# Attention scores with the second pass (q hi by K lo) as pairs of 64-row matmuls

## The chip, the cores and the metric

The kernel runs on one core of one Trainium2 chip. The metric is the device time of one execution in microseconds; a kernel's figure is the median of its runs.

## The reference, cut to what matters

Two residual blocks of a first kind run one after the other (1024 tokens, width 1024), then one block of a second kind (gated linear attention and a convolutional feed-forward). The change lies in the attention of the first kind, which is computed twice, once per layer:

```python
def gqa_axial_attention(q, k, v, qn_g, kn_g, tables):
    q = rmsnorm(q.reshape(b, s, H_B, HEAD_DIM), qn_g)      # 8 heads of 64
    k = rmsnorm(k.reshape(b, s, KV_HEADS, HEAD_DIM), kn_g) # 2 key heads of 64
    q = apply_axial_rope(q, tables)
    k = apply_axial_rope(k, tables)
    def attend(qblk):                                       # a block of 128 queries
        sc = jnp.einsum('bqkgd,bskd->bkgqs', qblk, k).astype(jnp.float32) * scale
        p = jax.nn.softmax(sc, axis=-1).astype(v.dtype)
        return jnp.einsum('bkgqs,bskd->bqkgd', p, v)
```

Everything is float32. For each block of 128 queries there are 2 key heads with 4 query heads each, and each of these 8 heads has a score matrix of 128 queries by 1024 keys.

## The kernel before, in words

**Numbers in two halves.** TensorE multiplies in the type fp32r. So that little is lost, the kernel writes a float32 number as a sum of two fp32r numbers, hi and lo (`split`, L71: a cast, on VectorE or ScalarE, and a subtraction on VectorE, L76 by way of L57), and adds up the products of the parts.

**The scores.** `qs` holds, for each head, 64 columns of q hi and 64 of q lo side by side (`split_q`, L411). A transpose of the 128 columns gives `qT`: rows 0 to 63 are q hi, rows 64 to 127 q lo (`prep_turn`, L414). `Kst` holds K hi (index 0) and K lo (index 1), each twice, in rows 0 to 63 and again in rows 64 to 127. So one matmul of 128 rows with K hi gives (q hi + q lo) by K hi, and a second one with K lo adds (q hi + q lo) by K lo. A score matrix `S` is 128 by 1024 floats in PSUM; there are two buffers of it. It takes four matmuls of 128x512: two column halves, each with K hi and then K lo (L476). Then VectorE takes the maximum of each row (`nm`, L481), ScalarE the exponential with a running sum (L66), which goes to SBUF and sets the buffer of `S` free.

**The loop.** Inside a layer the attention runs over g = 0 to 15 (8 query blocks qt by 2 key heads kv; g = 2 qt + kv), and for each g over eight units u0 to u7 (L591 and L598). In unit u TensorE does, in this order:

- `turn` (L493): four 128x128 transposes of exponentials of g into a PSUM tile named `tr`; ScalarE casts the tile to hi, VectorE subtracts for lo (tiles `X`);
- one piece of `scores(g+1)` (L467), as far as the next `yield`;
- at u2 `gate` (L510): two more transposes into a `tr` tile, which VectorE multiplies into `gb` (L517);
- at u1 `prep_turn` of g+2: four transposes into a `tr` tile, copied to `qT` by ScalarE;
- three matmuls of 128x512 of the output projection of the query block before (`project`, L547; tile `o`); when a column half is full, ScalarE squares it and VectorE multiplies it (`tmp`); after the second half `ss`, `ve`, a power on GpSimd (`rs`), and a VectorE operation over 128x1024 (`xt`, L567);
- at u7 of odd g `turn_ya`: four transposes into a `tr` tile;
- four matmuls of 128x256 with V (`attend`, L519; tile `po`), for the unit three earlier; after the last of eight, at u2 and u6, ScalarE copies half of `po` to `ol`, and VectorE adds (`ol`) and multiplies (`gb`).

**Who sets the order.** The order on TensorE is that of the program (L79, `manual_schedule`). On VectorE and ScalarE a scheduler sets it when the program is built, and the engine then runs its queue strictly in that order. There are two `tr` buffers for all the uses above; they are handed out in turn, so that transposes into a `tr` tile must wait until the reader of the tile two before is done. Only in the first query block do some units use the tile `o` in place of `tr` (L498).

Before the loop, `scores(0)` runs between pieces of `gate_b` (L574).

Of the kernel before, what the change touches and what calls it, by code (L numbers as in the profile page):

```python
# [11 lines left out]
AF = mybir.ActivationFunctionType  # L12
ALU = mybir.AluOpType
AX = mybir.AxisListType
# [22 lines left out]
def build(tc, a):  # L37
# [5 lines left out]
    nc = tc.nc  # L43
    seq = [0]

    def T(pool, shape, tag, dt=F32, bufs=None):
        seq[0] += 1
        return pool.tile(shape, dt, tag=tag, name=f"{tag}_{seq[0]}", bufs=bufs)

    def opened(stack, name, side="left"):  # L50
        return stack.enter_context(tc.tile_pool(name=name, bufs=1, side=side, reuse_waits="tile"))

    def opened_psum(stack, name):
        return stack.enter_context(tc.tile_pool(name=name, bufs=1, space=PSUM, reuse_waits="tile"))

    def tt(out, in0, in1, op, eng=None):
        (eng or nc.vector).tensor_tensor(out=out, in0=in0, in1=in1, op=op)  # L57
# [4 lines left out]
    def mm(out, lhsT, rhs, start, stop):  # L62
        nc.tensor.matmul(out, lhsT, rhs, start=start, stop=stop)  # L63

    def act(out, in_, func, **kw):
        nc.scalar.activation(out=out, in_=in_, func=func, **kw)  # L66
# [4 lines left out]
    def split(hi, lo, src, on_act=False):  # L71
        if on_act:
            nc.scalar.copy(hi, src)  # L73
        else:
            nc.vector.tensor_copy(hi, src)
        tt(lo, src, hi, ALU.subtract)  # L76
# [21 lines left out]
    def bcast(p, src, n, tag, bufs=1):  # L98
        t = T(p, [128, n], tag, bufs=bufs)
        load(t, src.broadcast_to([128, n]))  # L100
        return t
# [3 lines left out]
    def quarter(i, dt=F32R):  # L105

        return T(xpool, [128, 4096], f"X{i}", dt)
# [125 lines left out]
    for l in range(2):  # L233
        sP = ExitStack()
        psL = opened_psum(sP, f"psA{l}")
# [16 lines left out]
        if l == 0:  # L252
# [8 lines left out]
            for _ in range(2):  # L261
                for e in range(2):
                    r = identr[64 * e:64 * e + 64]
# [80 lines left out]
        Kst = T(pR, [128, 2, 2, 1024], "K", F32R)  # L344
# [6 lines left out]
        for i, nm, sc in ((1, "k_norm_g", 1.0), (0, "q_norm_g", 0.125)):  # L351
            g = bcast(pT, a[nm][l:l + 1, :], 64, "g64")
# [47 lines left out]
        qTs, qss = {}, {}  # L400

        def use_q(t, ps):
            qr = T(pT, [128, 512], "t1", bufs=2)
            rope(qr, T(pT, [128, 512], "sq", bufs=2), T(pT, [128, 512], "qn", bufs=2), ps, 8, 0, t)
            if t == 0:
                qss[0] = T(pT, [128, 8, 2, 64], "qs", F32R)
                split_q(0, qr)
            else:
                load(tok(q_d, t), qr)

        def split_q(qt, q):  # L411
            split(qss[qt][:, :, 0], qss[qt][:, :, 1], q.rearrange("p (h d) -> p h d", d=64))

        def prep_turn(g):  # L414
            qt, kv = divmod(g, 2)
# [31 lines left out]
        psL = opened_psum(sB, f"psB{l}")  # L447
        pB = opened(sB, f"pB{l}", "right")
        pQ = opened(sB, f"pQ{l}", "right")
        g_post = bcast(cst, a["post_g"][l:l + 1, :], 1024, "gpost")  # L450
        g_pre = bcast(cst, a["pre_g"][1:2, :] if l == 0 else a["norm1"], 1024, "gpre")
        XB = [x[:, j] for x in (quarter(i, F32).rearrange("p (u k) -> p u k", u=4) for i in (2, 3)) for j in range(4)]
        qf, ya = XB[7][:, 0:512], XB[7][:, 512:1024]
        count = [0, 0]
        Ps, gbs, pos, yTs = {}, {}, {}, {}
# [11 lines left out]
        def scores(g):  # L467

            qt, kv = divmod(g, 2)
            sm = T(pQ, [128, 4], "sm", bufs=3)  # L470
            P = {}
            for hh in (0, 2, 1, 3):
                ps = T(psL, [128, 1024], "S", bufs=2)
                for c in range(2):
                    for s in range(2):
                        mm(ps[:, 512 * c:512 * c + 512], qTs[g][:, hh],  # L476
                           Kst[:, s, kv, 512 * c:512 * c + 512], s == 0, s == 1)
                    if c == 0:
                        yield
                nm = T(pQ, [128, 1], "nm", bufs=4)  # L480
                nc.vector.reduce_max(out=nm, in_=ps, axis=AX.X, negate=True)  # L481
                P[hh] = XB[count[1] % 7]
                count[1] += 1
                act(P[hh], ps, AF.Exp, bias=nm, accum_out=sm[:, hh:hh + 1])
                if hh == 3:
                    ri = T(pQ, [128, 4], "ri", bufs=3)
                    nc.vector.reciprocal(ri, sm)
                    rb = T(pQ, [128, 4, 64], "rb")
                    nc.vector.tensor_copy(rb, ri.unsqueeze(2).broadcast_to([128, 4, 64]))
                    Ps[g] = P, rb  # L490
                yield

        def turn(g, u):  # L493

# [79 lines left out]
        for i, _ in enumerate(scores(0)):  # L574
            next(units[i // 4])
# [15 lines left out]
        for g in range(2 * NT):  # L591
            qt, kv = divmod(g, 2)
# [54 lines left out]
    cols = T(pG, [128, 3], "cols")  # L647
# [23 lines left out]
    def gmm(n=512, tag="mm"):  # L671
        return T(psG, [128, 512], tag, bufs=2)[:, 0:n]
# [86 lines left out]
    for h in range(4):  # L759
# [11 lines left out]
        for t in range(NT):  # L771
            if h == 0 and t == 6:
                alpha_low()
            ps = gmm(256, ("mm", "po")[t % 2])
# [15 lines left out]
        for hf in range(2):  # L790
            ps = gmm().rearrange("p (t i) -> p t i", t=4)
# [22 lines left out]
        for hf in range(2):  # L814
            ps = gmm().rearrange("p (t i) -> p t i", t=4)
# [16 lines left out]
        for t in range(NT):  # L832
            ps = gmm(256)
# [124 lines left out]
    for t in range(NT):  # L958
# [8 lines left out]
        for c in range(2):  # L967
            ps = T(psH, [128, 512], "mm", bufs=4)
# [227 lines left out]
    for c in range(2):  # L1196
        ps = [T(psD, [128, 512], f"d{t}") for t in range(NT)]
# [115 lines left out]
```

## Time and profile before

| | us |
|---|---|
| median of 3 runs | 2218.72 (2218.39 to 2222.95) |
| the profiled execution | 2216.28 |
| its span, first to last instruction | 2214.5 |
| TensorE matmuls busy in the span | 2185.2 (99%), 11919 matmuls |
| VectorE busy | 1511.8 (68%) |
| ScalarE busy | 927.5 (42%) |
| granted TensorE clock | 1.0 of full speed in all 40 slices |

The busy shares are means over the whole program. The two attention loops lie at about 279 to 530 us and 820 to 1072 us of the span, and for the change these stretches count: the transposes of `turn` and the score matmuls occur only there (the first score tile, before the loop, at 259 us). A matmul's busy time in the profile runs from its start to a modelled end, and matmuls overlap, so the price of one in a stream is the distance from its start to the next one's start.

### The profile page before, as it was taken

What the parts mean: (1) busy time and instruction counts of PE and PEld (TensorE: products, weight loads), DVE (VectorE), ACT (ScalarE), POOL (GpSimd) and SP (SyncE); (2) the same over time, 40 slices, a digit from 0 to 9 for tenths busy, and PEclk for the clock granted to TensorE, in tenths of its full rate; (3) what the DMA queues carried; (4) which work ended last, traced back from release to release, by engine and by line L of the source; (5) the groups of instructions that cost most, each with busy time, mean ns of one, the idle gap of its engine ahead of it and who ended that gap; (6) DMA issues with size and microseconds to landing.
All of it is one profiled execution on the core that took longest, in us unless ns stands there. A gap on an engine that the chain in (4) does not pass through costs nothing.

```text
span 2214.5 us, 30128 instructions
## 1 busy us (share of the span) xinstructions
PE 2185.2 (99%) x11919; PEld 1871.3 (85%) x11919; DVE 1511.8 (68%) x2307; ACT 927.5 (42%) x1631; POOL 157.1 (7%) x210
## 2 busy tenths in 40 slices
PE   8999999999999999999999999999999999999998
PEld 7888888888788878888889999988888888888887
DVE  7545688888844568888865555647998888763434
ACT  4203266666210326666643223223544444442323
POOL 1004200000100510000001001100000000000000
PEclk9999999999999999999999999999999999999999
DMA  5131411112423150111331111343222222264443
GB/s 196 62 120 39 148 39 63 44 53 90 144 68 105 39 162 25 58 48 49 113 108 49 53 57 63 107 161 107 77 86 86 86 81 81 77 225 147 147 148 122
DMA packets 74541, 206.52 MB, mean 93 GB/s; under 512 B 8736, under 2 KB 21408, under 8 KB 74400
## 3 DMA queue, kind: packets, MB, share of 16 engines
q1 hardware_dynamic: 73392, 200.93, 26.7%
q10 hardware_dynamic: 1008, 3.67, 0.6%
q8 instruction: 93, 1.52, 0.3%
q14 instruction: 48, 0.39, 0.1%
HBM read 160.01 MB, written 44.56 MB: 92 GB/s over the span
## 4 chain that ended last, share of the span: by engine, by line
PE 57%; DVE 5%; POOL 2%; issue 1%; ACT 1%; DMA 1%; POOLq 0%; SPq 0%; ACTq 0%; DVEq 0%
PE mm L63 13%; PE d L63 11%; PE a L1016 10%; PE b L1016 8%; PE po L63 5%; PE o L63 3%; PE S L63 3%; PE tr L504 2%; POOL rs L57 1%; DVE X L57 1%; POOL sq L57 1%; PE tr L154 1%; DVE w L57 0%; PE big L63 0%; PE tr L63 0%
## 5 line engine op out<-in xcount | busy, mean ns | idle before, releaser
L63 PE MATMUL mm<-w,X 128*128 128x512 f32 (+1 forms) x3072 | 550.6, 337 | 3.9 <-DVE w L57 1.8
L63 PEld LDWEIGHTS mm<-w,X 128*128 128x128 f32 x3072 | 475.5, 189 | 64.9 <-DVE w L57 2.6
L57 POOL TENSOR_TENSOR rs<-ve,nhalf 128x1 f32<-128x1 f32 (+2 forms) x136 | 109.6, 806 | 2025.1 <-DVE ve L93 2018.1
L63 PE MATMUL d<-w,X 128*128 128x512 f32 x1056 | 239.9, 389 | 0.1
L63 PEld LDWEIGHTS d<-w,X 128*128 128x128 f32 x1056 | 198.1, 188 | 41.7 <-DVE X L57 0.5
L57 DVE TENSOR_TENSOR X<-tr,X 128x512 fp32r<-128x512 f32 x296 | 201.5, 683 | 38.3 <-ACT X L73 35.3
L73 ACT CAST X<-tr 128x512 fp32r<-128x512 f32 x296 | 171.2, 585 | 114.2 <-PE tr L504 77.9
L57 DVE TENSOR_TENSOR w<-raw,w 128x1024 fp32r<-128x1024 f32 (+1 forms) x155 | 183.0, 1182 | 27.5 <-ACT w L73 26.5
L63 PE MATMUL S<-K,qT 128*128 128x512 f32 x512 | 179.0, 430 | 2.8 <-DVE t L60 1.6
L481 DVE TENSOR_REDUCE nm<-S 128x1 f32<-128x1024 f32 x128 | 155.7, 1217 | 25.5 <-PE S L63 25.1
L63 PEld LDWEIGHTS po<-X,V 128*128 128x128 f32 x1024 | 151.6, 189 | 22.8 <-DVE ol L57 6.8
L63 PE MATMUL po<-X,V 128*128 128x256 f32 x1024 | 167.6, 287 | 1.9 <-DVE ol L57 1.8
L66 ACT ACTIVATE X<-S,nm 128x1024 f32<-128x1024 f32 x128 | 143.0, 1117 | 62.0 <-DVE nm L481 61.8
L63 PE MATMUL mm<-X,w 128*128 128x512 f32 x672 | 155.5, 390 | 0.0
L1016 PE MATMUL a<-X,w 128*128 128x512 f32 x624 | 150.6, 393 | 0.8 <-DVE s L57 0.8
L504 PE MATMUL tr<-ident,X 128*128 128x128 f32 x960 | 144.7, 273 | 4.7 <-ACT qT L420 2.1
L63 PEld LDWEIGHTS mm<-X,w 128*128 128x128 f32 x672 | 125.3, 188 | 25.5
L57 DVE TENSOR_TENSOR X<-yr,X 128x1024 fp32r<-128x1024 f32 x44 | 53.6, 1221 | 135.1 <-ACT X L73 135.1
L1016 PEld LDWEIGHTS a<-X,w 128*128 128x128 f32 x624 | 117.1, 188 | 27.8 <-DVE s L57 1.3
L504 PEld LDWEIGHTS tr<-ident,X 128*128 128x128 f32 x960 | 110.6, 139 | 12.4 <-DVE X L57 3.9
L73 ACT CAST X<-yr 128x1024 fp32r<-128x1024 f32 x44 | 45.9, 1048 | 149.7 <-PE d L63 149.4
L66 ACT ACTIVATE t<-mm 128x512 f32<-128x512 f32 (+1 forms) x34 | 18.5, 543 | 210.8 <-PE mm L63 114.9
(272 smaller groups left out, 3288.4 us busy)
## 6 DMA issues: line engine op xcount, KB each, us to landing
raw<-w_in SPq DMA_DIRECT2D x46, 512.0 KB, 3.7
yr<-gs SPq DMA_DIRECT2D x44, 512.0 KB, 3.8
xt<-x SPq DMA_DIRECT2D x37, 512.0 KB, 3.6
raw<-gla_w_in SPq DMA_DIRECT2D x24, 512.0 KB, 3.6
raw<-w_up SPq DMA_DIRECT2D x22, 512.0 KB, 3.4
yr<-w_up SPq DMA_DIRECT2D x22, 512.0 KB, 3.5
gs<-s SPq DMA_DIRECT2D x22, 512.0 KB, 2.6
raw<-w_down SPq DMA_DIRECT2D x22, 512.0 KB, 4.4
```

The source lines that it names most:

```text
L57: (eng or nc.vector).tensor_tensor(out=out, in0=in0, in1=in1, op=op)
L63: nc.tensor.matmul(out, lhsT, rhs, start=start, stop=stop)
L66: nc.scalar.activation(out=out, in_=in_, func=func, **kw)
L73: nc.scalar.copy(hi, src)
L154: nc.tensor.transpose(ps[:, k], src[:, (j + k) * 128:(j + k + 1) * 128], ident)
L481: nc.vector.reduce_max(out=nm, in_=ps, axis=AX.X, negate=True)
L504: nc.tensor.transpose(ptr[:, k, e], P[pr + 2 * e][:, kt * 128:kt * 128 + 128], ident)
L1016: nc.tensor.matmul(ps, L[x], R[y], start=first and k == n == 0, stop=k == 3 and n == 2, skip_group_check=True)
```

## The change

The scores are computed for two heads at a time, hh = o and o + 2, for o = 0 and 1. For each of the two heads (e = 0, 1), two full matmuls with K hi come first. Then four matmuls of 64 rows each follow: head e = 0 uses rows 0 to 63 of `qT` and of `Kst`, head e = 1 rows 64 to 127, each for two column halves. `split_q` puts q lo in the first and q hi in the second half for the heads with e = 1, so that rows 64 to 127 are q hi there. The product q lo by K lo is not computed any more.

The points at which `scores` gives way to the rest of the unit move: of four units, the first has the K hi matmuls of head e = 0, the second those of e = 1, the third all four K lo matmuls and the softmax of e = 0, and the fourth no score matmul, only the softmax of e = 1.

```diff
         def split_q(qt, q):
-            split(qss[qt][:, :, 0], qss[qt][:, :, 1], q.rearrange("p (h d) -> p h d", d=64))
+
+            src = q.rearrange("p (v e o d) -> p v e o d", v=2, e=2, o=2)
+            dst = qss[qt].rearrange("p (v e o) s d -> p v e o s d", v=2, e=2)
+            for e in range(2):
+                split(dst[:, :, e, :, e], dst[:, :, e, :, 1 - e], src[:, :, e])
...
-            for hh in (0, 2, 1, 3):
-                ps = T(psL, [128, 1024], "S", bufs=2)
-                for c in range(2):
-                    for s in range(2):
-                        mm(ps[:, 512 * c:512 * c + 512], qTs[g][:, hh],
-                           Kst[:, s, kv, 512 * c:512 * c + 512], s == 0, s == 1)
-                    if c == 0:
-                        yield
-                nm = T(pQ, [128, 1], "nm", bufs=4)
-                nc.vector.reduce_max(out=nm, in_=ps, axis=AX.X, negate=True)
...
+            for o in range(2):
+                ps = [T(psL, [128, 1024], "S", bufs=2) for _ in range(2)]
+                cols = [slice(512 * c, 512 * c + 512) for c in range(2)]
+                for e in range(2):
+                    for c in cols:
+                        mm(ps[e][:, c], qTs[g][:, o + 2 * e], Kst[:, 0, kv, c], True, False)
+                    yield
+                for c in cols:
+                    for e in range(2):
+                        r = slice(64 * e, 64 * e + 64)
+                        mm(ps[e][:, c], qTs[g][r, o + 2 * e], Kst[r, 1, kv, c], False, True)
+                for e in range(2):
+                    hh = o + 2 * e
+                    nm = T(pQ, [128, 1], "nm", bufs=4)
+                    nc.vector.reduce_max(out=nm, in_=ps[e], axis=AX.X, negate=True)
...
```

What the change makes of the queues is shown at three places. The number behind a name tells one tile of that name from another; `X0` and `X1` are the split exponentials, and line numbers behind the diff are higher by 4 to 9 in the changed kernel.

TensorE, units u5 to u7 of an odd g, before:

```order
L504 MATMUL tr_717_4253<-ident_1_62,X2_351_2216 128x128 x4
L63 MATMUL S_716_4243<-K_192_1203,qT_667_3970 128x512 x2
L63 MATMUL o_711_4212<-w_328_2000,ya_688_4109 128x512 x3
L63 MATMUL po_714_4231<-X0_376_2333,V_193_1204 128x256 x4
L504 MATMUL tr_719_4272<-ident_1_62,X2_351_2216 128x128 x4
L63 MATMUL S_720_4279<-K_192_1203,qT_667_3970 128x512 x2
L63 MATMUL o_711_4212<-w5_330_2005,yb_707_4205 128x512 x3
L63 MATMUL po_714_4231<-X0_376_2333,V_193_1204 128x256 x4
L504 MATMUL tr_722_4293<-ident_1_62,X2_351_2216 128x128 x4
L63 MATMUL S_720_4279<-K_192_1203,qT_667_3970 128x512 x2
```

The same engine in the changed kernel, units u6 and u7 of an odd g and the start of the next u0 (`tr_754` is the tile of `turn_ya`):

```order
L513 MATMUL tr_746_4457<-ident_1_62,X3_352_2219 128x128 x4
L63 MATMUL S_743_4430<-K_192_1203,qT_698_4171 128x512
L63 MATMUL S_744_4431<-K_192_1203,qT_698_4171 128x512
L63 MATMUL S_743_4430<-K_192_1203,qT_698_4171 128x512
L63 MATMUL S_744_4431<-K_192_1203,qT_698_4171 128x512
L63 MATMUL o_738_4401<-w5_358_2232,yb_707_4221 128x512 x3
L63 MATMUL po_741_4418<-X0_376_2335,V_193_1204 128x256 x4
L513 MATMUL tr_749_4482<-ident_1_62,X3_352_2219 128x128 x4
L63 MATMUL o_738_4401<-w5_358_2232,yb_707_4221 128x512 x3
L154 MATMUL tr_754_4501<-ident_1_62,X3_352_2219 128x128 x4
L63 MATMUL po_755_4508<-X1_377_2336,V_193_1204 128x256 x4
L513 MATMUL tr_758_4522<-ident_1_62,X3_352_2219 128x128
```

Two score matmuls in every unit have become four in u6, alternating between two score tiles, and none in u7.

VectorE in the changed kernel over the same units (a query block's last four units):

```order
L57 TENSOR_TENSOR X1_377_2336<-tr_746_4457,X1_377_2336 128x512
L490 TENSOR_REDUCE nm_747_4468<-S_743_4430 128x1
L57 TENSOR_TENSOR ol_748_4478<-po_741_4418,ol_748_4478 64x256
L490 TENSOR_REDUCE nm_750_4489<-S_744_4431 128x1
L57 TENSOR_TENSOR gb_626_3755<-ol_748_4478,gb_626_3755 64x256
L57 TENSOR_TENSOR X1_377_2336<-tr_749_4482,X1_377_2336 128x512
L57 TENSOR_TENSOR ya_753_4500<-tr_754_4501,ya_753_4500 128x512
```

Both row maxima now stand ahead of the subtraction that reads `tr_749`, the tile of u7; before, one maximum stood before u6's subtraction and the next behind u7's.

VectorE at u2 and u3 of an even g, where the output projection of a query block ends, before:

```order
L57 TENSOR_TENSOR tmp_644_3833<-o_673_4008,gpost_349_2212 128x512
L57 TENSOR_TENSOR ss_700_4171<-ss2_645_3834 128x1
L93 TENSOR_SCALAR ve1_701_4173<-ss_700_4171 128x1
L60 SCALAR_TENSOR_TENSOR gb_626_3745<-gb_626_3745,tr_705_4193 128x256
L60 SCALAR_TENSOR_TENSOR xt_643_3831<-tmp_644_3833,rs1_702_4175,xt_643_3831 128x1024
L57 TENSOR_TENSOR ol_706_4201<-po_690_4117,ol_706_4201 64x256
L57 TENSOR_TENSOR X0_376_2333<-tr_703_4183,X0_376_2333 128x512
L57 TENSOR_TENSOR gb_561_3368<-ol_706_4201,gb_561_3368 64x256
L57 TENSOR_TENSOR X0_376_2333<-tr_712_4216,X0_376_2333 128x512
L481 TENSOR_REDUCE nm_713_4225<-S_704_4190 128x1
```

The same place in the changed kernel:

```order
L57 TENSOR_TENSOR tmp_709_4226<-o_738_4401,gpost_349_2214 128x512
L57 TENSOR_TENSOR ss_765_4562<-ss2_710_4227 128x1
L93 TENSOR_SCALAR ve1_766_4564<-ss_765_4562 128x1
L57 TENSOR_TENSOR X0_376_2335<-tr_768_4574,X0_376_2335 128x512
L60 SCALAR_TENSOR_TENSOR xt_708_4224<-tmp_709_4226,rs1_767_4566,xt_708_4224 128x1024
L57 TENSOR_TENSOR ol_771_4596<-po_755_4508,ol_771_4596 64x256
L490 TENSOR_REDUCE nm_769_4585<-S_760_4530 128x1
L60 SCALAR_TENSOR_TENSOR gb_691_4134<-gb_691_4134,tr_770_4588 128x256
L57 TENSOR_TENSOR gb_626_3755<-ol_771_4596,gb_626_3755 64x256
L57 TENSOR_TENSOR X0_376_2335<-tr_777_4611,X0_376_2335 128x512
L490 TENSOR_REDUCE nm_778_4618<-S_761_4531 128x1
L57 TENSOR_TENSOR yb_772_4600<-gb_626_3755,yb_772_4600 128x512
```

The gate's multiplication (`gb` from a `tr` tile) stood ahead of `xt`; it now stands behind `xt`, `ol` and the first row maximum, and the second row maximum follows two operations later.

## Rows read from the trace of the kernel before

**Rows 1.** The page, first part: busy time, share of the span, instructions by engine.

```profile
PE 2185.2 (99%) x11919; PEld 1871.3 (85%) x11919; DVE 1511.8 (68%) x2307; ACT 927.5 (42%) x1631; POOL 157.1 (7%) x210
```

**Rows 2.** Stretches: first query block, then a later one; busy by engine, clock, DMA.

```profile
279.50:299.50 20.00, 18.13 (x124) 15.36 (x123) 18.32 (x29) 15.12 (x29) 0.00 (x0) 1.00 0.11 31
...
334.50:369.50 35.00, 35.00 (x226) 30.89 (x225) 29.50 (x49) 23.22 (x44) 0.56 (x1) 1.00 0.16 54
```

**Rows 3.** Timeline of TensorE, one unit: start us, us, instruction, count.

```profile
307.69 0.60 PE L504 MATMUL tr<-ident,X 128*128 128x128 f32 x4
308.05 0.71 PE L63 MATMUL S<-K,qT 128*128 128x512 f32 x2
308.60 0.86 PE L63 MATMUL o<-w,ya 128*128 128x512 f32 x3
309.30 0.63 PE L63 MATMUL po<-X,V 128*128 128x256 f32 x4
```

**Rows 4.** Timelines of the warm-up at the start (L259 to L265), PE, PEld, DVE.

```profile
7.64 0.40 PE L63 MATMUL mm<-identr 128*128 128x512 f32 x1
...
7.97 0.50 PE L63 MATMUL mm<-identr 64*128 64x512 f32 x2
...
8.08 0.19 PEld L63 LDWEIGHTS mm<-identr 64*128 64x128 f32 x2
...
8.31 0.40 PE L63 MATMUL mm<-identr 64*128 64x512 f32 x2
...
8.63 0.14 PEld L154 LDWEIGHTS tr<-ident,xn 128*128 128x128 f32 x1 [0.37 <-DVE xn L60]
...
7.18 1.28 DVE L60 SCALAR_TENSOR_TENSOR xn<-xt,rs,gpre 128x1024 f32<-128x1024 f32 x1 [0.67 <-POOL rs L57]
```

**Rows 5.** Instruction groups by shape, 299.5 to 509.5 us: busy, mean ns, idle before.

```profile
L57 DVE TENSOR_TENSOR X<-tr,X 128x512 fp32r<-128x512 f32 x96 | 65.8, 685 | 17.1 <-ACT X L73 15.7
L481 DVE TENSOR_REDUCE nm<-S 128x1 f32<-128x1024 f32 x48 | 58.4, 1216 | 8.2 <-PE S L63 8.1
...
L73 ACT CAST X<-tr 128x512 fp32r<-128x512 f32 x96 | 56.1, 584 | 33.3 <-PE tr L504 31.8
L66 ACT ACTIVATE X<-S,nm 128x1024 f32<-128x1024 f32 x48 | 53.6, 1116 | 18.1 <-DVE nm L481 18.1
...
L66 ACT ACTIVATION_READ_ACCUMULATOR X<-S,nm 128x1 f32 x48 | 9.3, 194 | 0.0
L534 ACT COPY ol<-po 64x256 f32<-64x256 f32 x25 | 9.2, 367 | 3.3 <-PE po L63 2.9
...
L57 DVE TENSOR_TENSOR qs<-X,qs 128x512 fp32r<-128x512 f32 x5 | 3.4, 683 | 0.0
...
L75 DVE CAST qs<-X 128x512 fp32r<-128x512 f32 x5 | 2.1, 417 | 0.0
```

**Rows 6.** Timelines of TensorE and ScalarE around the transposes of one unit.

```profile
370.52 0.60 PE L504 MATMUL tr<-ident,X 128*128 128x128 f32 x4
...
371.21 0.59 ACT L73 CAST X<-tr 128x512 fp32r<-128x512 f32 x1 [0.38 <-PE tr L504]
...
374.74 0.60 ACT L66 ACTIVATE tmp<-o 128x512 f32<-128x512 f32 x1 [0.18 <-PE o L63]
```

**Rows 7.** Timeline of VectorE where a block's projection ends.

```profile
373.68 1.23 DVE L481 TENSOR_REDUCE nm<-S 128x1 f32<-128x1024 f32 x1 [0.24 <-PE S L63]
374.82 0.68 DVE L57 TENSOR_TENSOR X<-tr,X 128x512 fp32r<-128x512 f32 x1
375.46 0.69 DVE L57 TENSOR_TENSOR tmp<-o,gpost 128x512 f32<-128x512 f32 x1
...
376.25 0.15 DVE L93 TENSOR_SCALAR ve<-ss 128x1 f32<-128x1 f32 x1
376.33 0.42 DVE L60 SCALAR_TENSOR_TENSOR gb<-gb,tr 128x256 f32<-128x256 f32 x1
377.08 1.28 DVE L60 SCALAR_TENSOR_TENSOR xt<-tmp,rs,xt 128x1024 f32<-128x1024 f32 x1 [0.32 <-POOL rs L57]
378.39 0.43 DVE L57 TENSOR_TENSOR ol<-po,ol 64x256 f32<-64x256 f32 x1
```

More of the change, by code (lines that the diff above doesn't have):

```diff
@@ L471, in scores @@
             P = {}
-            for hh in (0, 2, 1, 3):
-                ps = T(psL, [128, 1024], "S", bufs=2)
-                for c in range(2):
-                    for s in range(2):
-                        mm(ps[:, 512 * c:512 * c + 512], qTs[g][:, hh],
-                           Kst[:, s, kv, 512 * c:512 * c + 512], s == 0, s == 1)
-                    if c == 0:
-                        yield
-                nm = T(pQ, [128, 1], "nm", bufs=4)
-                nc.vector.reduce_max(out=nm, in_=ps, axis=AX.X, negate=True)
[L482 to L491, printed above, removed]
+            for o in range(2):
[13 more added lines that the diff above has]
+                    nc.vector.reduce_max(out=nm, in_=ps[e], axis=AX.X, negate=True)
+                    P[hh] = XB[count[1] % 7]
+                    count[1] += 1
+                    act(P[hh], ps[e], AF.Exp, bias=nm, accum_out=sm[:, hh:hh + 1])
+                    if hh == 3:
+                        ri = T(pQ, [128, 4], "ri", bufs=3)
+                        nc.vector.reciprocal(ri, sm)
+                        rb = T(pQ, [128, 4, 64], "rb")
+                        nc.vector.tensor_copy(rb, ri.unsqueeze(2).broadcast_to([128, 4, 64]))
+                        Ps[g] = P, rb
+                    yield
         def turn(g, u):
```

## The prediction

> **What bounds the kernel now.** I read the page first: TensorE is busy 99% of the span, VectorE 68% [rows 1]. So a matmul that goes is worth its price, as long as nothing else is late. Whether that holds is a matter of the attention loops alone, and there the stretches say more than the page: a later query block takes 35.00 us, in which TensorE is busy throughout and VectorE 29.50 us, that is 84% [rows 2]. VectorE has 5.5 us to spare in each block, but its queue is strictly in order, so what counts is where in the queue an operation stands. The first query block, without a projection to fill TensorE, has VectorE at 18.32 of 20.00 us and TensorE at 18.13 [rows 2].
>
> A unit costs TensorE 2.07 us: transposes 0.36 us, then 0.55 for two score matmuls, 0.70 for three projection matmuls, 0.46 for four matmuls with V (start to start, [rows 3]). Of the 0.55, 0.08 belong to the change from transposes to other matmuls; I count 0.44 for transposes and 0.47 for two score matmuls, so 0.231 for one.
>
> **Part 1: the pairs.** Before the change four K lo matmuls of two heads cost 4 x 0.231 = 0.92 us. What four half matmuls cost, the warm-up shows, where L263 already issues two such pairs [rows 4]. The last full matmul starts at 7.64 and has streamed at 7.87. The first pair starts at 7.97, both at once, and its matmuls take 0.50 where the next take 0.40: the weight load, 0.10 us, stands in front of them. The second pair starts at 8.31, again both at once. So a pair does go for the price of one matmul, 0.23 us from stream to stream (8.07 to 8.31). But the next load of full size starts at 8.63, the same 0.33 us after the last pair as the first pair starts after the last full matmul, and not because its input was late: `xn` was done at 8.46. So there is a toll of some 0.2 us on the way in (7.87 to 8.07) and on the way out (8.54 to 8.63, and 0.10 for a load). Four half matmuls take 7.87 to 8.73 = 0.86 us, 0.06 less than before.
>
> The Trainium skill has a rule for each half of this. "TensorE: Matmul & The Clock Gate", Part 3, "Measured speedup vs the span model", has tiles side by side cost one matmul and about 4 ns per further tile; by that alone the four would take some 0.47 us. "TensorEngine Tiling (Array Packing)", "Key Properties", says that a change of tiling mode drains the engine, which speaks against a change that does it twice for two pairs; the warm-up's 0.33 us agree.
>
> There are 2 layers x 16 g x 2 = 64 such groups of two pairs: 64 x 0.06 = 3.8 us gained. From both sides: at best 0.46 per group, 64 x 0.46 = 29.6 us gained; at worst no overlap in the loop and the same tolls, 0.4 per group, 25.6 us lost. I take the warm-up's, the only rows with this form.
>
> **Part 2: what the new order makes late.** The K lo matmuls of both heads end together in the third of four units, so both row maxima and both exponentials come in one bunch, and the next K hi matmuls into the same two `S` tiles stand two units behind instead of three. I follow the queues with t = 0 when TensorE has streamed the transposes of that third unit. Steps from rows: ScalarE's cast starts 0.26 after t (transposes at 370.52, four of 0.108, cast at 371.21 [rows 6]) and takes 0.59; X subtraction 0.68, row maximum 1.22, exponential 1.12 and its accumulator read 0.19, overlapping by 0.1, copy of `po` 0.37 [rows 5]; VectorE lets an operation start about 0.08 before a row maximum ends (374.82 against 373.68 + 1.23) and likewise before one [rows 7]; 0.03 to 0.06 from engine to engine.
>
> *Last four units of odd g.* VectorE: X 0.88 to 1.56, first maximum to 2.70, `ol` to 3.12, second maximum to 4.26, `gb` to 4.60, X of u7 to 5.31. Only then is u7's `tr` buffer free, which the transposes of the next u0 need, because `turn_ya` took the other one. They can start at 5.37; TensorE is there at 0.86 + 0.70 + 0.46 + 0.44 + 0.70 + 0.44 + 0.46 = 4.06. Wait: 1.3 us.
>
> *First four units of even g.* The projection's last matmul has ended at -0.74; ScalarE's square and read, 0.60 + 0.19 [rows 6], let `tmp` run 0.07 to 0.76, `ve` to about 1.0; X to 1.73; `rs` is there 0.67 after `ve` (376.41 to 377.08 [rows 7]), so `xt` 1.76 to 3.04, `ol` to 3.50, first maximum to 4.64, and only now the gate's multiplication, to 4.98. Before, it stood ahead of `xt` [rows 7]. The transposes of u4 need its buffer: 5.04, against 0.86 + 0.21 + 0.46 + 0.70 + 0.44 + 0.70 + 0.46 = 3.83. Wait: 1.2 us. The exponential ends at 5.88, so the K hi matmuls of u4 start at 5.92, not 5.48: 0.4 more. `gb`, X and the second maximum end at 7.28, its exponential at 8.52; the K hi matmuls of u5 are due at 5.92 + 0.47 + 0.70 + 0.46 + 0.44 = 7.99 and start at 8.56: 0.6 more. Together 2.2 us.
>
> *Last four units of even g:* maximum to 2.70; ScalarE does u7's cast first, exponential to 4.43, K hi matmuls due at 4.06: 0.4 us. *First four of odd g:* no `xt`; the gate's multiplication is done at 3.71, in time; second maximum to 5.30 and its exponential to 6.54 against 6.4: 0.2 us. This holds the doubled number of `split_q` operations, which take 0.42 + 0.68 now [rows 5] and which I put at 1.2 us in four pieces.
>
> Sum per query block: 1.3 + 2.2 + 0.4 + 0.2 = 4.1 us. TensorE has no slack in a block now [rows 2], so each wait lengthens it. The queues have the same order for blocks 2 to 7 of both layers, 12 times: 49 us. Blocks 0 and 1 are different: in block 0 VectorE is nearly full and the bunching may cost up to 5 us a layer, or nothing, since three buffers serve the transposes there; I take nothing and keep 10 us for the range. The K lo price hardly matters now: were the pairs cheaper, TensorE would only come earlier to the same waits. VectorE's total does not rise by more than the 0.1 us of `split_q` per block; the pieces before the loop (`scores(0)`) have 1.4 us matmuls of `gate_b` between them and gain or lose nothing that I can see.
>
> **Sum.** The profiled execution took 2216.28 us (span 2214.5 and 1.8 around it), 2.4 less than the median of the runs shown. 2216.3 - 3.8 + 49 = 2261.5, so I say 2262 us, 2.0% slower.
>
> **The rivals.** *Faster, as the title says.* Two matmuls side by side without tolls and all waits hidden: 2216.3 - 29.6 = 2187. For it: pairs do start at the same time [rows 4]. Against: the toll in the same rows, and a VectorE queue in which five operations stand between a transposition and the release of its buffer. It would need both; the rule on tiles side by side in the Trainium skill ("TensorE: Matmul & The Clock Gate", Part 3) is this case. Its point: each chain above would have to end 1.2 us earlier, a whole row maximum. Chance 0.06.
>
> *No change.* Tolls as measured, but the waits hidden: 2216.3 - 3.8 = 2212.5, or with the tolls of a slower exit up to 2220. For it: TensorE waits on VectorE hardly at all today. Against: the release points move by 3 us and more in the queue. The part of it within 0.2% has 0.04.
>
> *Half of the waits.* Only the chain with `xt` bites, since it hangs on the longest operations; the other waits lie within what overlap of neighbours on VectorE and ScalarE can take back: 12 x 2.2 - 3.8 = +23, so 2239. Chance 0.18.
>
> *More.* No overlap around the row maxima, 1 us more per block (12 us), and block 0 pays 5 us a layer: 2262 + 22 = 2284. Chance 0.15. If TensorE's clock fell in the new gaps it would be worse still; in the first stretch of [rows 2] TensorE idles 1.9 of 20 us at a full clock.
>
> **How the numbers follow.** The forecast itself has the remaining 0.57, and spreads by some 10 us for the estimates in the chains. About 0.2% (4.4 us) is what a measurement of this kernel can tell from no change. Faster by more: 0.06; within: 0.04; slower: 0.57 + 0.18 + 0.15 = 0.90. The range reaches down to the half of the waits and up to the case of more, 2236 to 2288; outside lie the two cases that are not slower and the worst of the last. The two bounds of the pairs' price lie inside it, as long as the waits are there: 5 us per layer at most is left of a cheaper pair, since only the waits of 0.4 and 0.2 us would give way.
>
> **What would show it.** A query block of 38.5 to 40 us in place of 35.00, with VectorE's busy time still near 29.5. In the waits, transposes (`tr`) waiting on VectorE's `gb` and `X`, and `S` waiting on ScalarE's exponential, some 25 us in each layer. In the timeline a pair of 64-row matmuls starting together, the next pair 0.33 us later and the next full load 0.33 us after that. I am wrong if blocks stay at 35 us or less; if the groups of four half matmuls take 0.5 us; or if TensorE's idle time falls on other tiles than `tr` and `S`.

## The result

The changed kernel takes 2279.64 us (median of 4 runs, 2278.83 to 2280.42), the kernel before 2218.90 us: 1.027 times as long, interval 1.0252 to 1.0287. It is slower, as forecast. The time lies inside the range, and 18 us above the 2262 us that I gave.

The page of the changed kernel, first part and two of the costliest groups (span 2277.0 us), the counterpart of [rows 1] (busy us, share of the span and instructions; then busy and mean ns, and idle time in front with its releaser):

```profile
PE 2203.8 (97%) x11919; PEld 1846.7 (81%) x11919; DVE 1516.6 (67%) x2339; ACT 926.4 (41%) x1631; POOL 156.3 (7%) x210
...
L513 PE MATMUL tr<-ident,X 128*128 128x128 f32 x960 | 147.1, 276 | 29.1 <-DVE X L57 15.1
...
L63 PE MATMUL S<-K,qT 128*128 128x512 f32 (+1 forms) x512 | 139.4, 445 | 20.4 <-ACT X L66 17.4
```

The span has grown by 62.5 us. VectorE works nearly as long as before (1516.6 us against 1511.8), each row maximum takes what it took (1215 ns against 1216, [rows 5]), and the number of matmuls is the same. What is new is idle time of TensorE, 73.2 us in place of 29.3, and it stands in front of two kinds of work: transposes, 29.1 us (4.7 before), most of it waits on VectorE, and score matmuls, 20.4 us (2.8 before), most of it waits on ScalarE. The other 18.6 us of the growth the page counts as busy, in part because a matmul's modelled end reaches into a wait behind it (below).

The waits of TensorE over most of one loop, 300 to 530 us of the changed kernel (total us, times, longest):

```profile
PE S L63 <- ACT X L66: 6.0, 13, 1.8
PE tr L513 <- DVE X L57: 5.3, 6, 0.9
PE tr L513 <- DVE gb L60: 4.8, 5, 1.0
```

Where do they fall? The transposes of `turn_ya` (L154) run once per query block, so the distance from one to the next is the length of a block. First and a later block of the kernel before, then of the changed one (columns as in [rows 2]):

```profile
299.68:334.66 34.98, 34.22 (x220) 29.77 (x218) 28.30 (x46) 23.23 (x44) 0.00 (x0) 1.00 0.08 24
439.52:474.46 34.94, 34.94 (x225) 30.84 (x224) 29.45 (x48) 23.22 (x44) 0.55 (x1) 1.00 0.14 46
```

```profile
305.45:342.09 36.64, 34.79 (x219) 28.13 (x219) 27.98 (x47) 22.89 (x43) 0.00 (x0) 1.00 0.07 23
458.62:497.49 38.87, 36.20 (x225) 29.18 (x224) 29.75 (x50) 23.11 (x45) 0.55 (x1) 1.00 0.13 41
```

A later block is longer by 3.9 us with VectorE's work the same to 0.3 us: the block is not full on VectorE, it is out of step. Adding up one layer from the starts of these transposes (the last column is the second layer):

| stretch | before | changed | longer by, layer 0 | layer 1 |
|---|---|---|---|---|
| block 0, to its `turn_ya` | at 299.68 | at 305.45 | 5.8 | 5.4 |
| block 1 | 34.98 | 36.64 | 1.7 | 1.6 |
| blocks 2 to 6 | 174.84 | 194.33 | 19.5 | 19.5 |
| rest of the loop and its tail | 35.31 | 39.88 | 4.6 | 4.5 |
| sum, before rounding | | | 31.5 | 30.9 |

The sum of both layers, 62.4 us, is all but 0.1 us of the difference in span.

**The waits of one block.** The block from 458.62 us on, TensorE, at the four places that the prediction spoke of (start, us, instructions, in brackets idle before):

```profile
460.63 0.66 PE L513 MATMUL tr<-ident,X 128*128 128x128 f32 x4 [0.93 <-DVE X L57]
...
470.75 0.66 PE L513 MATMUL tr<-ident,X 128*128 128x128 f32 x4 [0.97 <-DVE gb L60]
...
474.30 0.73 PE L63 MATMUL S<-K,qT 128*128 128x512 f32 x2 [0.42 <-ACT X L66]
...
480.95 0.50 PE L63 MATMUL S<-K,qT 128*128 128x512 f32 x1 [0.17 <-ACT X L66]
```

The idle time in brackets counts from the modelled end of the matmul before, which lies some 0.16 us behind the end of its stream, so a wait costs 0.16 more than the bracket. Measured by start against start, the six waits are 1.09 (u0), 1.13 (u4), 0.29 and 0.58 (`S` of u4 and u5), 0.34 (`S` at u0 of the odd g) and 0.21 us (transposes at u5 of the odd g, 491.65), together 3.64. And this is VectorE in front of the first of them, the order that the change makes:

```profile
456.34 0.69 DVE L57 TENSOR_TENSOR X<-tr,X 128x512 fp32r<-128x512 f32 x1 [1.50 <-ACT X L73]
456.95 1.22 DVE L490 TENSOR_REDUCE nm<-S 128x1 f32<-128x1024 f32 x1
458.09 0.42 DVE L57 TENSOR_TENSOR ol<-po,ol 64x256 f32<-64x256 f32 x1
458.43 1.21 DVE L490 TENSOR_REDUCE nm<-S 128x1 f32<-128x1024 f32 x1
459.56 0.41 DVE L57 TENSOR_TENSOR gb<-ol,gb 64x256 f32<-64x256 f32 x1
459.89 0.68 DVE L57 TENSOR_TENSOR X<-tr,X 128x512 fp32r<-128x512 f32 x1
```

VectorE idles 1.50 us, waiting for ScalarE's cast of a `tr` tile, then has both maxima close together, and the subtraction that frees u7's `tr` buffer stands behind them; it ends at 460.57, and at 460.63 the transposes start.

**The pairs.** A group of pairs in the same block, from narrow cuts of the timeline (so the counts are of the matmuls that lie in the cut):

```profile
465.41 0.38 PE L513 MATMUL tr<-ident,X 128*128 128x128 f32 x2
465.72 0.50 PE L63 MATMUL S<-K,qT 64*128 64x512 f32 x2
...
466.05 0.40 PE L63 MATMUL S<-K,qT 64*128 64x512 f32 x2
466.38 0.33 PE L524 MATMUL tr<-ident,rb 128*128 128x128 f32 x1
```

Two matmuls start together at 465.72, two at 466.05, and the next work of full size follows at 466.38: 0.33 us twice, as in the warm-up [rows 4].

### The profile page after: what moved, and what is told of

It reads as the page before. It is cut to its first block, busy times and chain, and to the rows that moved or that the text cites. A ratio compares the mean times of both kernels' runs of the same rounds, so it can differ in the third digit from the quotient of the medians.

```text
span 2277.0 us, 30120 instructions
## 1 busy us (share of the span) xinstructions
PE 2203.8 (97%) x11919; PEld 1846.7 (81%) x11919; DVE 1516.6 (67%) x2339; ACT 926.4 (41%) x1631; POOL 156.3 (7%) x210
## 4 chain that ended last, share of the span: by engine, by line
PE 79%; DVE 12%; ACT 4%; issue 2%; POOL 1%; DMA 1%; SPq 0%; POOLq 0%; ACTq 0%; DVEq 0%
PE mm L63 32%; PE d L63 10%; PE a L1025 10%; PE b L1025 8%; PE po L63 5%; PE S L63 4%; DVE nm L490 4%; PE o L63 3%; PE tr L513 3%; DVE X L57 2%; ACT X L66 2%; ACT X L73 1%; PE tr L154 1%; POOL rs L57 1%; DMA raw<-w_in 1%
## 5 line engine op out<-in xcount | busy, mean ns | idle before, releaser
L513 PE MATMUL tr<-ident,X 128*128 128x128 f32 x960 | 147.1, 276 | 29.1 <-DVE X L57 15.1
L490 DVE TENSOR_REDUCE nm<-S 128x1 f32<-128x1024 f32 x128 | 155.2, 1215 | 7.6 <-PE S L63 6.8
L63 PE MATMUL S<-K,qT 128*128 128x512 f32 (+1 forms) x512 | 139.4, 445 | 20.4 <-ACT X L66 17.4
```

What stands on the lines that cost most here:

```text
L490: nc.vector.reduce_max(out=nm, in_=ps[e], axis=AX.X, negate=True)
L513: nc.tensor.transpose(ptr[:, k, e], P[pr + 2 * e][:, kt * 128:kt * 128 + 128], ident)
```

## The experiments

Twelve kernels were run. "The changed kernel" is the base of a diff unless the text says otherwise; block lengths are of the same steady block.

**The order without the pairs.** K lo as four full matmuls in the changed kernel's order, with the old `split_q`.

```diff
                 for c in cols:
                     for e in range(2):
-                        r = slice(64 * e, 64 * e + 64)
-                        mm(ps[e][:, c], qTs[g][r, o + 2 * e], Kst[r, 1, kv, c], False, True)
+                        mm(ps[e][:, c], qTs[g][:, o + 2 * e], Kst[:, 1, kv, c], False, True)
```

> The new order alone: scores in pairs of heads as in the changed kernel, but the four K lo matmuls are full ones of 128 rows, and split_q is as before. If the waits come from the order (both row maxima and both exponentials in one bunch), the time stays near the changed kernel's 2280: the chains on VectorE start from the transposes and do not know what a K lo matmul costs, so 2276 to 2286. If instead the 64-row form with its drain on the way in and out is what costs, the time returns to 2216 to 2230.

Measured: 2283.35 us (2282.07 to 2284.91), 1.0284 (1.0269 to 1.03) of before. Its block, and TensorE's waits in that block:

```profile
459.52:498.50 38.98, 36.35 (x226) 30.94 (x225) 29.82 (x48) 23.14 (x45) 0.55 (x1) 1.00 0.13 41
```

```profile
PE tr L509 <- DVE gb L60: 1.0, 1, 1.0
PE tr L509 <- DVE X L57: 0.9, 1, 0.9
PE S L63 <- ACT X L66: 0.6, 2, 0.4
```

Without a single matmul of 64 rows the block is as long and waits at the same places for the same times. VectorE's order in it is that of the changed kernel, but for the two more operations of `split_q`. The order is the cause of the loss, and the pairs win back some 0.1 us of a block. (Between the same neighbours the four groups of 64-row matmuls are 0.04 to 0.12 us shorter than four full ones, 0.3 together; part of that is waited away again behind them. The spans say less here: of the 6.2 us by which this run's is longer, 3.75 lie between the two loops, at 577.46 to 856.85 us, where this execution's mean granted clock was 0.99 and the changed kernel's 1.00.)

**The pairs' toll without the order.** The kernel before, head by head, with the K lo pass on rows 0 to 63 alone and not in pairs (the product q lo by K lo is left out, as in the change). Eight visits to the 64-row form per block in place of four.

```diff
-                for c in range(2):
-                    for s in range(2):
-                        mm(ps[:, 512 * c:512 * c + 512], qTs[g][:, hh],
-                           Kst[:, s, kv, 512 * c:512 * c + 512], s == 0, s == 1)
-                    if c == 0:
+                for s in range(2):
+                    r = slice(0, 64 if s else 128)
+                    for c in range(2):
+                        mm(ps[:, 512 * c:512 * c + 512], qTs[g][r, hh],
+                           Kst[r, s, kv, 512 * c:512 * c + 512], s == 0, s == 1)
+                    if s == 0:
                         yield
```

> The 64-row form alone, one head at a time and with no partner: per head two full K hi matmuls in one unit, two K lo matmuls of rows 0 to 63 in the next, the rest as before (q lo by K lo is left out). TensorE bound, with two matmuls of 0.23 us each and a toll of 0.2 us in and 0.2 us out per visit: 128 visits x 0.4 = 51 us more than before, 2267, between 2250 and 2275. If the form is free, 2216 to 2220. Nothing on VectorE is bunched here, so the waits of the changed kernel should be missing.

Measured: 2261.25 us (2258.73 to 2264.34), 1.0185 (1.0168 to 1.0202). A block of it, and TensorE around one visit:

```profile
453.68:491.39 37.71, 37.71 (x225) 30.54 (x224) 29.96 (x48) 23.08 (x44) 0.55 (x1) 1.00 0.14 43
```

```profile
475.83 0.73 PE L63 MATMUL S<-K,qT 64*128 64x512 f32 x2
476.49 0.53 PE L419 MATMUL tr<-identr,qs 128*128 128x128 f32 x4
```

Here TensorE is busy for the whole block and still 2.77 us longer: 0.35 us for each of eight visits. That is the toll of going into the 64-row form and out again, close to the 0.4 of the prediction. The visit has two half matmuls one after the other, and takes 0.66 us from its start to the next work (475.83 to 476.49), as the changed kernel's two pairs do (465.72 to 466.38): in a pair the second matmul is free. So a group of two pairs saves two streams, 0.46 us, and pays 0.35: 0.1 us, on 64 groups at most 7 us of the whole program. The pairs have next to nothing to give here, before any wait.

**K hi of both heads later.** The first of four units has no score matmul, the second the K hi matmuls of both heads, so that they stand farther from the exponentials of the pair before.

```diff
                 cols = [slice(512 * c, 512 * c + 512) for c in range(2)]
+                yield
                 for e in range(2):
                     for c in cols:
                         mm(ps[e][:, c], qTs[g][:, o + 2 * e], Kst[:, 0, kv, c], True, False)
-                    yield
+                yield
```

> The changed kernel, but the K hi matmuls of both heads go together into the second of four units, so that every score buffer is written again three units after its K lo matmul, as before the change, in place of two. If the short distance to the reuse of the score buffers is the cause, most of the loss goes: 2216 to 2235. If the bunch on VectorE is the cause, only the wait of 0.4 us at the end of each even g goes, 12 x 0.4 = 5 us: 2270 to 2278.

Measured: 2280.26 us (2278.16 to 2283.59), 1.0271 (1.0256 to 1.0287). The block is 38.95 us, and the waits move from tile to tile:

```profile
PE tr L514 <- DVE X L57: 1.4, 2, 0.9
PE tr L514 <- DVE gb L60: 1.0, 1, 1.0
PE S L63 <- ACT X L66: 0.8, 1, 0.8
```

My expectation of 2270 to 2278 was missed. `S` waits once in place of twice, and the transposes wait 2.4 us in place of 1.9. I read this as TensorE coming earlier to a wait for `tr` that ends when VectorE's subtraction does; no run tests it.

**The new `split_q` alone**, in the kernel before.

```diff
-            split(qss[qt][:, :, 0], qss[qt][:, :, 1], q.rearrange("p (h d) -> p h d", d=64))
+            src = q.rearrange("p (v e o d) -> p v e o d", v=2, e=2, o=2)
+            dst = qss[qt].rearrange("p (v e o) s d -> p v e o s d", v=2, e=2)
+            for e in range(2):
+                split(dst[:, :, e, :, e], dst[:, :, e, :, 1 - e], src[:, :, e])
```

> The kernel before with the new split_q alone (four smaller VectorE operations in place of two, hi and lo swapped for half the heads). Off the path: 0 to 2 us more than before, 2217 to 2221. If the strided halves cost on the path, some 0.5 us per block, 2224 and more.

Measured: 2221.00 us (10 runs), 1.000 (0.9991 to 1.001). The two more operations per block are hidden.

**A shorter row maximum.** Both kernels with the maximum over 512 of 1024 columns. (Half of the row maximum is left out, and the exponent is scaled by 0.85 so that it stays in range; the softmax is another one.)

```diff
-                    nc.vector.reduce_max(out=nm, in_=ps[e], axis=AX.X, negate=True)
+                    nc.vector.reduce_max(out=nm, in_=ps[e][:, 0:512], axis=AX.X, negate=True)
...
-                    act(P[hh], ps[e], AF.Exp, bias=nm, accum_out=sm[:, hh:hh + 1])
+                    act(P[hh], ps[e], AF.Exp, bias=nm, scale=0.85, accum_out=sm[:, hh:hh + 1])
```

In the changed kernel:

> The changed kernel with the row maximum taken over 512 of the 1024 columns, and a factor of 0.85 in the exponential so that it stays finite; so the softmax is not the reference's. VectorE's row maximum takes about 0.6 us less, and the scheduler sets both maxima closer together. If the chain through both row maxima holds the transposes, the wait at the end of each query block falls from 1.3 to near 0 and those at u4 and u5 of even g from 2.2 to about 1.0; per block 3 us less, 12 x 3 = 37, and some us in the first blocks: 2225 to 2245. If the 64-row matmuls' toll is the loss, no change: 2275 to 2285.

In the kernel before, with the same edit:

> Control: the same halved row maximum and factor in the kernel before, whose softmax is not the reference's either. TensorE is the bound there, so VectorE's shorter queue is worth nothing: 2214 to 2221.

Measured: 2262.41 us (2261.26 to 2264.03) for the changed kernel, 1.0194 (1.0177 to 1.0211); 2233.34 us (2 runs) for the kernel before, 1.0063 (1.0043 to 1.0083). Both expectations were missed, and the second shows why the first says little. A block of the changed kernel with the short maximum, then one of the kernel before with it:

```profile
450.77:488.95 38.18, 35.96 (x225) 29.18 (x224) 25.76 (x49) 23.37 (x45) 0.55 (x1) 1.00 0.12 42
```

```profile
441.08:476.82 35.74, 35.22 (x225) 31.01 (x224) 25.76 (x48) 22.78 (x44) 0.55 (x1) 1.00 0.14 45
```

Both have 3.7 to 4.0 us less work on VectorE. One block is 0.7 us shorter, the other 0.8 us longer. The scheduler sees another duration and builds another order: in both kernels VectorE's queue differs from the one without the edit at several places of the block. So this pair doesn't measure what a maximum costs; it does show that less work on VectorE is not enough to shorten a later block. The first block is another matter. With the short maximum the first `turn_ya` of the changed kernel starts at 299.27 us in place of 305.45, and 12.0 of the 15.8 us by which the span is shorter lie in the two first blocks. There, where VectorE was busy for 18.32 of 20.00 us already before the change [rows 2], its work may well count; how much of the 12 us is the other order stays open.

**The projection one unit earlier.** If the wait of u4 is the chain `tmp`, `rs`, `xt`, first maximum, gate, then starting the projection at u1 in place of u2 should loosen it.

```diff
-                if kv == 0 and u == 2 and qt > 0:
+                if kv == 0 and u == 1 and qt > 0:
```

> The changed kernel with the output projection of a query block begun at u1 in place of u2, so that it ends a unit earlier and its 1.28 us operation on VectorE (xt) stands ahead of the bunch of both row maxima, and the gate's multiplication directly behind the first maximum. If xt in that bunch makes the waits of 2.2 us at u4 and u5 of even g, they go: 12 x 2.2 = 26 us less, 2250 to 2260. The wait of 1.3 us at the end of the block stays. If the toll is the cause, no change: 2275 to 2285.

Measured: 2266.09 us (2265.51 to 2268.11), 1.0212 (1.0197 to 1.0228). The block and its waits:

```profile
454.94:492.17 37.23, 35.75 (x226) 29.11 (x224) 29.58 (x50) 22.88 (x45) 0.55 (x1) 1.00 0.13 43
```

```profile
PE tr L513 <- DVE X L57: 0.9, 1, 0.9
PE S L63 <- ACT X L66: 0.5, 2, 0.3
```

The wait for `gb` is gone and the block 1.64 us shorter; the wait of u0 behind both maxima is untouched. The chain with `xt` was named rightly. The time fell by 13.5 us and not by the 20 to 30 that I expected: block 2 gained 1.4 us, blocks 0 and 1 lost 0.9 between them, and the rest of the loop gained 0.5.

**The same with more room.** Also `attend` one unit later, and a higher priority for the cast and the subtraction of `turn` and the gate's multiplication in the engines' queues.

```diff
-GU, PU, YU, LAG = 2, 1, 7, 3
+GU, PU, YU, LAG = 2, 1, 7, 4
...
-            split(PT[:, 0], PT[:, 1], ptr, on_act=True)
+            with tc.high_priority(HO):
+                split(PT[:, 0], PT[:, 1], ptr, on_act=True)
...
-            stt(gr, gr, 0.5, pr_, ALU.mult, ALU.mult)
+            with tc.high_priority(HO):
+                stt(gr, gr, 0.5, pr_, ALU.mult, ALU.mult)
...
-                if kv == 0 and u == 2 and qt > 0:
+                if kv == 0 and u == 1 and qt > 0:
```

> As the kernel before it in this list, and besides with the V matmuls four units behind the transposes in place of three, and the readers of the transposition tiles (subtraction and gate) raised in the scheduler's priority. The queue then has the gate ahead of both maxima and neither xt nor the last additions between them; left is a wait of about 0.5 us at the end of a block. 2216 - 4 + 12 x 0.5 = 2218 for the later blocks, and up to 10 us for the first ones: 2214 to 2230. If bunching cannot be worked round by order, 2245 and more.

Measured: 2273.79 us (2272.34 to 2277.69), 1.0248 (1.0233 to 1.0264). The theory's own forecast for this run failed. Waits of TensorE in a block of 37.75 us:

```profile
PE S L63 <- ACT X L66: 0.8, 3, 0.3
PE tr L513 <- DVE X L57: 0.3, 1, 0.3
```

By the start-against-start count the transposes wait 0.7 us in this block in place of 2.4, and the score matmuls 1.2 at three places, as much as in the changed kernel. So the waits on VectorE gave way and those on ScalarE's exponentials did not; the block is still 2.8 us longer than before, and three things were changed at once, so that none of them is priced here.

**`turn_ya` at u5**, so that the `tr` buffer of u7 is not the one that the next u0 needs; alone, then with the earlier projection, then with K hi later as well.

```diff
-GU, PU, YU, LAG = 2, 1, 7, 3
+GU, PU, YU, LAG = 2, 1, 5, 3
```

> The changed kernel with turn_ya moved from u7 to u5 of odd g, one number. VectorE's queue at the end of a block stays: two maxima ahead of the subtraction for u7. But the transposes of the next u0 now need the tile of u6, not of u7, so the wait of 1.1 us goes and the next one shows: the K hi matmuls of u0 wait some 0.4 us for the exponential. 12 x 0.7 = 9 us less: 2268 to 2274. If the wait is not one for the transposition tile, no change, 2278 to 2282.

> The one before and the projection begun at u1, which took 13.5 us off the changed kernel alone. If the waits are separate and add up, 2280 - 13.5 - 9 = 2257, between 2252 and 2262. If VectorE's total is the bound of the block, the second gain is lost: 2264 to 2268.

> The one before and the K hi matmuls of both heads in the second of four units, three units after the last K lo matmuls instead of two. Alone this was worth nothing, since the transposition tiles held the block. If the short distance is the next thing to bind, the remaining waits of 0.35 to 0.45 us for the exponential go now: 12 x 1.2 = 14 us less, 2238 to 2248. If the distance does not matter here either, 2255 to 2260.

Measured: 2274.27 us (2272.05 to 2277.60), 1.0246 (1.023 to 1.0261); 2262.19 us (2261.08 to 2262.61), 1.019 (1.0173 to 1.0207); 2260.13 us (2259.04 to 2262.05), 1.0182 (1.0166 to 1.0197). The first two stand a few tenths above what the theory expected of them; the third was to reach 2238 to 2248 and did not. A block of it:

```profile
449.20:485.70 36.50, 36.04 (x225) 28.74 (x224) 29.23 (x49) 22.56 (x44) 0.55 (x1) 1.00 0.13 44
```

The large waits that the prediction named are gone, and the block is still 1.6 us longer than before. By the same start-against-start count, 1.1 us of it are four smaller waits: two of `po` matmuls on VectorE's `ol` (0.41 at 463.08, 0.21 at 481.16), a place that the prediction did not name, and two of transposes on VectorE's `X` (0.26 at 465.51, 0.24 at 483.59). Of the 21.2 us that this kernel loses in the first layer, 10.0 lie in the six blocks from one `turn_ya` to the next, and 11.1 before the first and behind the last. It is the fastest of the variants with pairs, and 40 us behind the kernel before.

**The first query block in the old order.** `scores(0)` to `scores(2)` of each layer, which run before and in the first block, as they were; all others in pairs.

```diff
+            if g < 3:
+                for hh in (0, 2, 1, 3):
+                    ps = T(psL, [128, 1024], "S", bufs=2)
+                    for c in range(2):
+                        for s in range(2):
+                            mm(ps[:, 512 * c:512 * c + 512], qTs[g][:, hh],
+                               Kst[:, s, kv, 512 * c:512 * c + 512], s == 0, s == 1)
+                        if c == 0:
+                            yield
...
+                return
```

> The changed kernel, but scores(0), scores(1) and scores(2) of each layer, the three that are computed before and during the first query block, in the form and order of before; all others in pairs as changed. If the bunched order is what makes the first block longer, the first Y of a layer comes back from 305.4 to about 300 us, the waits of 1.8 us of S on ScalarE in it and the fall of the granted clock at 303 us go, and the time is 2279.6 - 2 x 5.6 = 2268 (2264 to 2272), with the blocks from the third on still near 38.9 us. Rival: the first block is held by something else (VectorE's queue as the scheduler makes it, with or without the pairs), then it stays at 2276 to 2282. In both cases block 1 may change by 2 us a layer either way.

Measured: 2269.88 us (2269.38 to 2270.94), 1.0223 (1.0209 to 1.0237). The first `turn_ya` starts at 300.11 us in place of 305.45, and the later block keeps its 38.88:

```profile
300.11:336.11 36.00, 34.41 (x219) 28.05 (x218) 27.97 (x47) 21.87 (x41) 0.00 (x0) 1.00 0.07 23
452.97:491.85 38.88, 36.20 (x226) 29.16 (x225) 29.75 (x50) 23.10 (x45) 0.55 (x1) 1.00 0.13 41
```

So the bunched order, with its pairs, costs the first block its 5.3 us, and the cost stays where the order stays. The pairs are not needed for it: the run with the order alone has its first `turn_ya` at 305.77 us. Waits of TensorE in the first block, in the changed kernel (279.5 to 305.5 us), then in this one (279.5 to 300 us):

```profile
PE S L63 <- ACT X L66: 4.4, 3, 1.8
PE po L63 <- DVE ol L57: 2.2, 2, 1.1
```

```profile
PE po L63 <- DVE ol L57: 0.9, 1, 0.9
PE o L535 <- DVE X L57: 0.6, 2, 0.4
PE S L63 <- ACT X L66: 0.6, 2, 0.4
```

## Why the prediction was right, and where it was off

**That VectorE's order and not its load decides: right.** Busy time the same to 0.3 us per block, block longer by 3.9; the run with the order alone has all of it.

**Part 1, the pairs: right in form, a little too dear.** The pairs start together, and the next pair and the next full work follow 0.33 us later, as forecast. I took 0.4 us of toll per visit; the run with eight visits per block measures 0.35. The two rules of the Trainium skill that I had weighed now both have their run. The Trainium skill, "TensorEngine Tiling (Array Packing)", "Key Properties", says that a change of tiling mode drains the engine; the trace agrees, with 2.77 us more per block while TensorE is busy throughout. The Trainium skill, "TensorE: Matmul & The Clock Gate", Part 3, "Measured speedup vs the span model", has tiles side by side cost one matmul and about 4 ns per further tile. The trace agrees on the pair, whose second matmul starts 4 ns behind its first at 465.72, and not on the group, which takes 0.66 us to the next work where the prediction worked out 0.47 by that rule.

**Part 2, the waits of a steady block: right at five of six places, in size partly by luck.** Forecast against measured: u0 behind both maxima 1.3 and 1.09; u4 behind `xt`, `ol` and a maximum 1.2 and 1.13; `S` of u4 and u5 together 1.0 and 0.87; `S` behind the end of the even g 0.4 and 0.34. For the odd g the prediction had 0.2 for `S` behind an exponential; the 0.21 measured are transposes that wait for VectorE's subtraction behind the second maximum. Together 4.1 and 3.64. The block grew by 3.9, though the pairs take some 0.3 off it. What is missing is the start-up behind each wait, which the prediction did not have: counted as far as the second matmul behind it, against the same steps of the kernel before, the six waits are 1.15, 1.19, 0.39, 0.69, 0.44 and 0.39, together 4.2 us, of which the kernel before has 0.2 in its own block. So the waits were forecast 0.5 us too long and 0.6 us of start-up was left out; that the two cancel is luck. Blocks 2 to 7 of a layer: 6 x (4.1 - 0.24) = 23.2 forecast, 19.5 + 4.6 = 24.1 measured.

**Blocks 0 and 1: the step that failed.** The prediction says of block 0 "I take nothing and keep 10 us for the range", because three buffers serve the transposes there, and says nothing more of block 1. Measured are 5.8 and 1.7 us in layer 0, 5.4 and 1.6 in layer 1: 14 us in all, most of the 18 by which the number was short. The third buffer helps the transposes only. What waits in block 0 is `S`, which has two buffers there as elsewhere, and `po`: 4.4 and 2.2 us, against 0.6 and 0.9 in the kernel before (279.5 to 299.7 us). In block 1 of layer 0 it is `S` again, 1.2 us against none before. Some 1 us of each first block goes with a fall of the clock (last section). TensorE in the changed kernel, then ScalarE:

```profile
296.36 0.74 PE L63 MATMUL po<-X,V 128*128 128x256 f32 x4 [1.10 <-DVE ol L57]
...
300.74 0.74 PE L63 MATMUL S<-K,qT 128*128 128x512 f32 x2 [1.84 <-ACT X L66]
```

```profile
299.48 1.12 ACT L66 ACTIVATE X<-S,nm 128x1024 f32<-128x1024 f32 x1
300.49 0.20 ACT L66 ACTIVATION_READ_ACCUMULATOR X<-S,nm 128x1 f32 x1
```

The exponential that frees `S` has its last part done at 300.69, and at 300.74 the score matmuls start. A unit without projection is 0.7 us shorter on TensorE [rows 3], so that the matmuls come sooner to the same release; and VectorE, which makes the maximum that the exponential needs, is nearly full there, to which the run with the short maximum fits. The prediction had the row for this, 18.32 of 20.00 us on VectorE [rows 2], and its case of more, 5 us per layer for block 0, was the price that came; I should have taken it into the sum, by the same walk through the queues that priced the later blocks.

**Rivals.** Faster, no change and half of the waits are out. Of *more*, the part on block 0 came; its 1 us more per block did not.

**Still open.** Why the best variant keeps 1.6 us per block was read from its waits and not tested. In block 0, what the order costs and what VectorE's fuller queue costs are not separated: the short maximum changed both.

## What to carry to other kernels

Before a matmul is split into pairs of half the rows, count the visits to that form: each costs 0.35 us here, and two pairs save 0.46. If matmuls are bunched to make pairs, so is all that reads them: follow each in-order queue through one period, and price every buffer that is freed behind the bunch, the ramp-up blocks too. An engine at 84% of a stretch is no reserve when its operations come two at a time.

## What the chip showed that I had not expected

TensorE's clock fell in the first block of each layer of the changed kernel, where the kernel before keeps full clock. Two stretches of the first layer:

```profile
300.00:303.00 3.00, 2.26 (x12) 1.80 (x14) 0.30 (x1) 1.09 (x3) 0.00 (x0) 0.85 0.00 0
303.00:306.00 3.00, 3.00 (x17) 2.41 (x14) 2.24 (x3) 0.81 (x3) 0.00 (x0) 0.58 0.00 0
```

A granted clock of 0.58 is mostly the lower of the two levels, 1.2 GHz. TensorE had idled 1.10 us up to 296.36 and 1.84 us up to 300.74. The lost clock, 3 x 0.15 + 3 x 0.42 = 1.7 us, bounds its part of block 0's 5.8 us from above. The run with `turn_ya` at u5 alone tells more. From the first transposes of `turn` to the first `turn_ya`, VectorE and ScalarE have the same order in both layers, and TensorE the same waits (4.4 us for `S`, 2.2 for `po`), but the clock fell in the first layer only:

```profile
274.18:302.74 28.56, 21.29 (x138) 17.10 (x136) 22.32 (x37) 18.11 (x33) 0.00 (x0) 0.94 0.22 65
853.14:880.40 27.26, 19.96 (x137) 15.92 (x136) 22.32 (x37) 18.11 (x33) 0.00 (x0) 1.00 0.22 68
```

The block with the fall is 1.3 us longer. In two other variants, where also just one layer's first block has it, the difference is 0.7 (projection earlier, with more room) and 0.9 us (all three edits). So some 1 us of block 0's 5.8 goes with the clock, an estimate from these three differences, and the rest is waits.

The run with the old first block kept its clock there, and lost it later, in the next part of the program, where transposes of `xn` wait on VectorE:

```profile
602.00:604.00 2.00, 0.15 (x1) 0.00 (x0) 2.00 (x4) 0.28 (x1) 0.00 (x0) 1.00 0.49 197
604.00:611.50 7.50, 6.18 (x19) 4.90 (x20) 7.36 (x15) 2.97 (x6) 1.65 (x3) 0.54 0.38 132
```

This is 7.5 x 0.46 = 3.5 us, and that run's span is 7.8 us shorter than the changed kernel's, though its two first blocks alone are 10.5 us shorter. In the kernel before, TensorE is busy 0.76 of 3.00 us at the same place (576.4 to 579.4 us) at full clock. Nor does it take an edit: the kernel before itself took 2216.33 us in one execution, at a mean granted clock of 0.999, and 2223.03 us in another, at 0.996. So a few microseconds of a difference need a look at the clock before they are put down to an edit.
